# Two decoder layers: up-projection as 512- plus 256-column passes in four banks, banded attention by two heads on the two halves of the array's rows

## The chip, the cores and the metric

The kernel runs on one core of a Trainium2 chip. The time is the device time of one execution in microseconds (us); where several runs are given, their median is used. The engines are named as in the profile: PE is TensorE's matmuls, PEld its weight loads, DVE is VectorE, ACT is ScalarE, POOL is GpSimd, SP is the engine that issues the DMAs.

## The reference, cut to what matters

Batch 1, 256 tokens, model width 2048, two layers, everything in float32.

```
for l in range(2):
    shift_a, scale_a, gate_a, shift_m, scale_m, gate_m = split(silu(c) @ w_ada[l] + b_ada[l])
    h = rms_norm(x, g_pre_mix) * (1 + scale_a) + shift_a
    q_m, k_m, v_m, o_m, i, f, q_a, k_a, v_a = split(h @ w_in)      # one projection
    hm = mlstm(silu(conv(q_m, k_m)), v_m, i, f), normed, * sigmoid(o_m)
    ha = rms_norm(sliding_window_attention(q_a, k_a, v_a, sinks))
    x = x + gate_a * rms_norm(concat(hm, ha) @ w_out)
    h = rms_norm(x, g_pre_mlp) * (1 + scale_m) + shift_m
    x = x + gate_m * rms_norm(relu(h @ w_up)^2 @ w_down)           # 2048 -> 8192 -> 2048
```

The attention has 16 query heads of width 64 and 4 key heads; a query sees the last 128 keys. With blocks of 128 tokens its scores are, for each head, one 128x128 block (first tokens) and one 128x256 block (second tokens against both key blocks); a slope times the distance is subtracted, a sink logit joins the softmax.

## The kernel before, in words

**The split.** A float32 product is made of three products of a rounded type (float32r): each operand is a high part (h, the value rounded) and a low part (l, the rest), and high*high, low*high and high*low are added up in PSUM. Weights come by DMA in loads of 1 MB (`raw`, six buffers, issued by SP in the order of a list `plan`). `split` (lines 222 to 238) makes of half a load one slab: ACT copies 128x1024 into `whi` (line 232), DVE subtracts into `wlo` (line 236). There are four buffers of each, and `prefill` keeps the splits up to three slabs ahead of the matmuls. A slab is two steps of 128 along the contraction (kt) by 512 output columns.

**Units.** `Unit` (lines 287 to 324) is one block of 512 output columns over all kt, with two PSUM banks. PSUM has eight banks: four of `ps_mm` for units and four of `ps_x` for all else, whose users are counted in `live["x"]`; a unit made with `spare=True` takes its banks from `ps_x`. `slabs` issues for each slab the splits ahead, then one step of every open `Task` (`side`), then the slab's matmuls. So side work is bound to the pace of the slabs, each engine working off what it is handed in the order written by the compiler's scheduler. `body_xs` (line 332) keeps activations as the stationary operand and streams 512 weight columns; `body_ws` (line 337) keeps 128 columns of weights and streams the 256 tokens, so a kt step has 4 column groups j with three matmuls of 256 columns each: whi with xh, whi with xl, wlo with xh. Two groups j share a bank.

**Modulation.** `ada_op` (line 198) makes the adaLN values on DVE, one 128x2048 product-and-sum (line 204) for each 1 MB of `w_ada`. `weave` spreads these between the slabs; layer 0's MLP carries 64 of them, layer 1's 32.

**Mixer.** After the projection units for values, keys and queries, `swa` (line 646) runs the attention as a side task while the other projection units (qm, km, vm, om) run. It starts one head per slab, at most four in flight; `swa_head` (line 584) takes one step per slab: scores on the PE (lines 591, 592; 64 partitions, those of the head's half), mask and maxima on DVE (595 to 600), exponentials on ACT (602, 603), three transposes (609), copy (612), the product with the values (618 to 620). Four heads share a PSUM tile `po`, and the next four start when it is done. `mlstm_out` and `concat` wait for the attention's end, and the output projection `op` for `concat`.

**MLP.** `turn` starts the first up units (four in layer 0, two in layer 1) while the norm still runs. Then for each e of 8: `up(2e+2)`, four down units `down(e, c)` of 4 slabs with 512-column matmuls, `up(2e+3)` of 8 slabs (lines 1086 to 1101). `evac_up` (line 1009) takes a finished up unit out of PSUM in two steps: ACT relu and square, DVE square and difference, into the high and low parts that `down` uses one e later.

Of the kernel before, what the change touches and what calls it, by code (L numbers as in the profile page):

```python
# [16 lines left out]
P = 128  # L17
D = 2048
KT = D // P
S = 256  # L20
# [19 lines left out]
def hymba_kernel(ctx: ExitStack, tc: tile.TileContext, x_d, c_d, cols_d, cons_d, wada_d,  # L40
# [243 lines left out]
    def xdone(n=1):  # L284
        live["x"] -= n

    class Unit:


        def __init__(self, name, unit, nk, act, body, spare=False):  # L290
            self.unit, self.nk, self.act, self.body, self.spare = unit, nk, act, body, spare
            self.started = [False, False]
            if spare:
                self.ps = [xalloc(f"{name}_{b}") for b in range(2)]
            else:
                self.ps = [ps_mm.tile([P, 512], F32, tag="mm", name=f"{name}_{b}") for b in range(2)]

# [75 lines left out]
    class PreNorm:  # L373
# [35 lines left out]
        def group(self, g, tok):  # L409

            tag, l = self.tag, self.l
            ada_until(l, self.vsc, self.vsh, n=4 * g + 4)
            if g not in self.groups:
                self.groups[g] = [htp.tile([P, 4, S], F32R, tag=f"ht{a}", name=f"ht{a}{tag}_{g}") for a in "hl"]
            hh, hl = [t[:, :, TK[tok]] for t in self.groups[g]]
# [27 lines left out]
        def modulate(self, e, xnT, hfp):  # L443
# [3 lines left out]
            if g not in self.groups:  # L447
                self.groups[g] = [htp.tile([P, 4, S], F32R, tag=f"ht{a}", name=f"ht{a}{tag}_{g}") for a in "hl"]
            hh, hl = [t[:, 2 * (e % 2):2 * (e % 2) + 2, :] for t in self.groups[g]]
            hf = hfp.tile([P, 2, S], F32, tag="r", name=f"hfs{tag}_{e}")  # L450
# [11 lines left out]
        def __call__(self, kt):  # L462
            hh, hl = self.groups[kt // 4]
            return hh[:, kt % 4, :], hl[:, kt % 4, :]

# [58 lines left out]
    for l in range(DEPTH):  # L524
# [58 lines left out]

        def swa_head(h, po):
            u, hh = h // 8, h % 8
            base, j = 64 * (hh // 4), hh % 4
            qt = fl["qa", u][base:base + 64, j, :]
            kt_ = kaT[base:base + 64, u, :]
            live["w"] += 1
            pss = xalloc(f"pss{L}_{h}")  # L590
            T.matmul(pss[:, 0:P], qt[:, TK[0]], kt_[:, TK[0]], start=True, stop=True)  # L591
            T.matmul(pss[:, P:3 * P], qt[:, TK[1]], kt_, start=True, stop=True)  # L592
            yield
            s = walloc(f"s{L}_{h}", 0)
            V.scalar_tensor_tensor(s, dist, -(2.0 ** (-8.0 * (h + 1) / 16.0)), pss[:, 0:384],
                                   ALU.mult, ALU.add)
            xdone()
            V.tensor_reduce(mx[:, h, 0:1], s[:, 0:P], AX.X, ALU.max)
            V.tensor_reduce(mx[:, h, 1:2], s[:, P:384], AX.X, ALU.max)
            V.tensor_scalar(nm[:, h, :], mx[:, h, :], sk[:, h:h + 1], -1.0, ALU.max, ALU.mult)  # L600
            yield
            A.activation(s[:, 0:P], s[:, 0:P], AF.Exp, bias=nm[:, h, 0:1], accum_out=sm[:, h, 0:1])
            A.activation(s[:, P:384], s[:, P:384], AF.Exp, bias=nm[:, h, 1:2], accum_out=sm[:, h, 1:2])
            yield
            while live["x"] > 3:
                yield
            pt = xalloc(f"pt{L}_{h}")
            for b in range(3):
                T.transpose(pt[:, b * P:(b + 1) * P], s[:, b * P:(b + 1) * P], ident)
            yield  # L610
            sT = walloc(f"sT{L}_{h}", 0)
            A.activation(sT, pt[:, 0:384], AF.Copy)
            xdone()
            yield
            vs = slice((h // 4) * 64, (h // 4) * 64 + 64)
            c0 = (h % 4) * 64
            o0, o1 = po[:, c0:c0 + 64], po[:, 256 + c0:256 + c0 + 64]
            T.matmul(o0, sT[:, 0:P], vat[:, 0, vs], start=True, stop=True)
            T.matmul(o1, sT[:, P:2 * P], vat[:, 0, vs], start=True, stop=False)
            T.matmul(o1, sT[:, 2 * P:3 * P], vat[:, 1, vs], start=False, stop=True)  # L620
            live["w"] -= 1

        def swa_out(g, po):

            hs = slice(4 * g, 4 * g + 4)
            for b in range(2):
                V.tensor_tensor(es[:, hs, b], nm[:, hs, b], sk[:, hs], ALU.add)
            A.activation(es[:, hs, :], es[:, hs, :], AF.Exp)
            V.tensor_tensor(sm[:, hs, :], sm[:, hs, :], es[:, hs, :], ALU.add)
            V.reciprocal(sm[:, hs, :], sm[:, hs, :])  # L630
            yield
            o0 = (g % 2) * 256
            for b in range(2):
                if g % 2 == 0:
                    ha[g // 2, b] = ytile(f"ha{L}_{g // 2}_{b}")
                o = ha[g // 2, b][:, o0:o0 + 256]
                V.tensor_tensor(o.rearrange("p (h d) -> p h d", h=4),
                                po[:, b * 256:b * 256 + 256].rearrange("p (h d) -> p h d", h=4),
                                sm[:, hs, b:b + 1].broadcast_to([P, 4, 64]), ALU.mult)
            xdone()  # L640
            yield
            for b in range(2):
                square_sum(ha[g // 2, b][:, o0:o0 + 256], ssa[:, b, g:g + 1], f"jka{L}_{g}_{b}")
            yield

        def swa():
            while ("qa", 0) not in fl or "kv" not in fl:
                yield
            fly, nxt, outs, po = [], 0, [], None
            while nxt < 16 or fly or outs:  # L650
                for f in list(fly):
                    try:
                        next(f[0])
                    except StopIteration:
                        fly.remove(f)
                        live["q"] -= f[1] % 8 == 7
                        if f[1] % 4 == 3:
                            outs.append(swa_out(f[1] // 4, f[2]))
                            po = None
                for o in list(outs):  # L660
                    try:
                        next(o)
                    except StopIteration:
                        outs.remove(o)
                ok = nxt < 16 and len(fly) < 4 and ("qa", nxt // 8) in fl
                if ok and nxt % 4 == 0:
                    ok = po is None and live["x"] <= 1
                    if ok:
                        po = xalloc(f"po{L}_{nxt // 4}")
# [222 lines left out]
        def concat(i):  # L892
# [8 lines left out]

            hh, hl = [htp.tile([P, 4, S], F32R, tag=f"ht{a}", name=f"ct{a}{L}_{i}") for a in "hl"]
            for q in range(2):
# [105 lines left out]
        def evac_up(un, u):  # L1009
            ps = un.ps  # L1010
            sh, sl = s_tiles(u)
            for b in range(2):
# [8 lines left out]
                yield  # L1021

        def evac_up_tokens(un, u):

# [45 lines left out]

        def evac_down_task(ps, e, c):
            for tok in range(2):
                evac_down(ps, e, c, tok)
            yield

        def down(e, c):
# [4 lines left out]
            if c == 0:  # L1081
                tups[2 * e].finish()
                tups[2 * e + 1].finish()
            return Unit(f"dn{L}_{e}_{c}", ("dn", l, (e, c)), 8, hs, body_xs)

        for e in range(8):
# [5 lines left out]
            for c in range(4):  # L1092
                un = down(e, c)
                if (e, c) == (7, 3):
                    break
                td = Task(evac_down_task(un.run(), e, c))
            if e < 7:
# [108 lines left out]
```

## Time and profile before

| | |
|---|---|
| median of 3 runs | 2267.68 us (2267.40 to 2269.11) |
| the profiled execution | 2270.54 us |
| its span, first to last instruction | 2268.8 us |
| PE / PEld / DVE / ACT busy | 96% / 85% / 74% / 48% of the span |
| chain that ended last: PE / DVE / ACT | 86% / 10% / 2% |
| matmul instructions | 13322 |
| moved from HBM | 586 MB, 259 GB/s over the span |

Read the chain first: it says which engine's work followed on which up to the end. PE's busy time alone says little, since matmuls overlap in the records: a 256-column matmul is recorded with 283 ns, but they start every 120 ns. The spacing of the starts, which the chain gives as a piece's length over its matmuls, is what one costs.

### The profile page before, as it was taken

What the parts mean: (1) busy time and instruction counts of PE and PEld (TensorE: products, weight loads), DVE (VectorE), ACT (ScalarE), POOL (GpSimd) and SP (SyncE); (2) the same over time, 40 slices, a digit from 0 to 9 for tenths busy, and PEclk for the clock granted to TensorE, in tenths of its full rate; (3) what the DMA queues carried; (4) which work ended last, traced back from release to release, by engine and by line L of the source; (5) the groups of instructions that cost most, each with busy time, mean ns of one, the idle gap of its engine ahead of it and who ended that gap; (6) DMA issues with size and microseconds to landing.
All of it is one profiled execution on the core that took longest, in us unless ns stands there. A gap on an engine that the chain in (4) does not pass through costs nothing.

```text
span 2268.8 us, 33092 instructions
## 1 busy us (share of the span) xinstructions
PE 2180.5 (96%) x13322; PEld 1935.3 (85%) x13322; DVE 1688.3 (74%) x2282; ACT 1091.1 (48%) x1533; POOL 1.4 (0%) x14
## 2 busy tenths in 40 slices
PE   6889999899999999999989999989999999999998
PEld 4779777698898998989869988878898998998986
DVE  7988899788788777887577887957556656555556
ACT  4246654645444444434465566546443444444433
POOL 0000000000000000000000000000000000000000
PEclk9999999999999999999999999999999999999999
DMA  9997679488888888888539765745666667555551
GB/s 364 383 364 264 229 299 350 188 343 317 315 303 345 310 308 319 314 317 308 193 118 338 292 236 204 291 172 204 223 223 225 226 225 270 205 186 186 186 188 72
DMA packets 82363, 590.08 MB, mean 260 GB/s; under 512 B 9185, under 2 KB 9633, under 8 KB 10785
## 3 DMA queue, kind: packets, MB, share of 16 engines
q1 hardware_dynamic: 82210, 587.98, 69.6%
q8 instruction: 104, 1.70, 0.3%
q14 instruction: 49, 0.40, 0.1%
HBM read 585.81 MB, written 2.13 MB: 259 GB/s over the span
## 4 chain that ended last, share of the span: by engine, by line
PE 86%; DVE 10%; ACT 2%; issue 1%; DMA 0%; SPq 0%; DVEq 0%; ACTq 0%
PE up L329 32%; PE dn L329 30%; PE op L329 6%; DVE raw L204 4%; PE vm L329 3%; PE om L329 3%; PE qa L329 3%; DVE wlo L236 2%; PE km L329 2%; PE qm L329 2%; PE kva L329 1%; DVE x L388 1%; PE pss L592 1%; PE pss L591 1%; PE psgate L730 0%
## 5 line engine op out<-in xcount | busy, mean ns | idle before, releaser
L236 DVE TENSOR_TENSOR wlo<-raw,whi 128x1024 fp32r<-128x1024 f32 x720 | 876.5, 1223 | 456.8 <-ACT whi L232 455.7
L232 ACT ACTIVATE whi<-raw 128x1024 fp32r<-128x1024 f32 x720 | 758.5, 1058 | 899.1 <-PE dn L329 358.6
L329 PE MATMUL up<-hthm,whi 128*128 128x256 f32 x1920 | 543.6, 283 | 0.0
L329 PE MATMUL up<-hthm,wlo 128*128 128x256 f32 x1920 | 543.3, 283 | 0.0
L329 PE MATMUL up<-htlm,whi 128*128 128x256 f32 x1920 | 543.3, 283 | 0.0
L204 DVE SCALAR_TENSOR_TENSOR raw<-raw,cact 128x2048 f32<-128x2048 f32 x192 | 437.5, 2286 | 8.4 <-DMA raw<-in_wada_dram 8.2
L329 PE MATMUL dn<-whi,sh 128*128 128x512 f32 x1024 | 398.7, 389 | 0.0
L329 PE MATMUL dn<-whi,sl 128*128 128x512 f32 x1024 | 398.6, 389 | 0.0
L329 PE MATMUL dn<-wlo,sh 128*128 128x512 f32 x1024 | 398.4, 389 | 0.0
L329 PEld LDWEIGHTS up<-hthm,whi 128*128 128x128 f32 x1920 | 368.5, 192 | 0.8
L329 PEld LDWEIGHTS up<-htlm,whi 128*128 128x128 f32 x1920 | 368.5, 192 | 0.8
L329 PEld LDWEIGHTS up<-hthm,wlo 128*128 128x128 f32 x1920 | 368.5, 192 | 0.0
L329 PEld LDWEIGHTS dn<-wlo,sh 128*128 128x128 f32 x1024 | 192.2, 188 | 40.1
L329 PEld LDWEIGHTS dn<-whi,sh 128*128 128x128 f32 x1024 | 192.3, 188 | 39.7 <-ACT sh L1036 0.4
L329 PEld LDWEIGHTS dn<-whi,sl 128*128 128x128 f32 x1024 | 192.3, 188 | 39.5 <-DVE sl L1037 0.2
L329 PE MATMUL op<-wlo,cth 128*128 128x512 f32 x256 | 99.6, 395 | 3.1 <-DVE wlo L236 3.0
L329 PE MATMUL op<-whi,cth 128*128 128x512 f32 x256 | 99.3, 396 | 2.4 <-ACT whi L232 2.4
L329 PE MATMUL op<-whi,ctl 128*128 128x512 f32 x256 | 100.2, 393 | 0.0
L329 PE MATMUL vm<-whi,htha 128*128 128x512 f32 x128 | 57.1, 448 | 27.9 <-ACT whi L232 18.0
L1066 DVE TENSOR_TENSOR ys<-ys,dn 128x512 f32<-128x512 f32 x112 | 75.2, 686 | 4.3 <-PE dn L329 4.3
L329 PE MATMUL qa<-htha,whi 128*128 128x256 f32 x256 | 73.2, 286 | 0.0
L329 PE MATMUL qa<-htla,whi 128*128 128x256 f32 x256 | 72.4, 283 | 0.0
(275 smaller groups left out, 2551.3 us busy)
## 6 DMA issues: line engine op xcount, KB each, us to landing
raw<-in_wada_dram SPq DMA_DIRECT2D x192, 1024.0 KB, 6.2
raw<-in_wdn_dram SPq DMA_DIRECT2D x128, 1024.0 KB, 5.1
raw<-in_wup_dram SPq DMA_DIRECT2D x120, 1024.0 KB, 4.9
raw<-in_win_dram SPq DMA_DIRECT2D x56, 1024.0 KB, 5.5
raw<-in_wout_dram SPq DMA_DIRECT2D x32, 1024.0 KB, 6.5
raw<-in_wst_dram SPq DMA_DIRECT2D x16, 1024.0 KB, 7.3
raw<-in_wsu_dram SPq DMA_DIRECT2D x8, 1024.0 KB, 6.8
gp<-gdr SPq DMA_DIRECT2D x4, 1024.0 KB, 4.6
```

Source lines behind the costliest of these rows:

```text
L204: V.scalar_tensor_tensor(w, w, 1.0, cact, ALU.mult, ALU.mult, accum_out=modc[l][:, v, j:j + 1])
L232: A.activation(hi, raw, AF.Copy)
L236: V.tensor_tensor(lo, raw, hi.bitcast(F32), ALU.subtract)
L329: T.matmul(o, a, w, start=not self.started[b], stop=last and i == 2, skip_group_check=True)
L388: V.scalar_tensor_tensor(xc, self.yg[c][tok], r, xc, ALU.mult, ALU.add)
L591: T.matmul(pss[:, 0:P], qt[:, TK[0]], kt_[:, TK[0]], start=True, stop=True)
L592: T.matmul(pss[:, P:3 * P], qt[:, TK[1]], kt_, start=True, stop=True)
L1066: V.tensor_tensor(yt, yt, ps[tok], ALU.add)
```

## The change

In words:

1. Activations' high and low parts lie in one tile, 4 x 2 x 256 per group (`both_parts`), so that for one kt the high and low tokens are 512 adjacent columns. The memory is the same.
2. `body_wide` replaces `body_ws` for the up units made by `up(u)` (12 in layer 0, 14 in layer 1): for each kt and j one 512-column matmul of whi with [xh, xl] and one 256-column matmul of wlo with xh into the first half. Each j has a bank of its own, so a unit has four banks; `up` takes the four of `ps_x` for odd u and for u = 2, else the four of `ps_mm`. The down units with e > 0 and c < 2 take their two from `ps_x`.
3. `evac_up_wide` must add the two halves: per bank ACT copies the second half (256 columns) and DVE adds the first; then DVE makes relu times the value, ACT copies the high part, DVE subtracts.
4. `swa_pair` runs head h and head h+4, whose queries and keys lie on partitions 0 to 63 and 64 to 127, together: both heads' matmuls of the same block follow one another. A pair starts when `live["x"]` is at most 2, at most three pairs are in flight, two pairs share a `po`. `swa_out` and the loop are reordered to match.

```diff
+    def both_parts(name):
+        return htp.tile([P, 4, 2, S], F32R, tag="ht", name=name)
...
+    def body_wide(u, xh, xl, wh, wl, kt):
+        for j in range(4):
+            cs = slice(j * P, (j + 1) * P)
+            T.matmul(u.ps[j], wh[:, cs], u.act.both(kt), start=kt == 0, stop=False, skip_group_check=True)
+            T.matmul(u.ps[j][:, 0:S], wl[:, cs], xh, start=False, stop=kt == u.nk - 1, skip_group_check=True)
...
+        def swa_pair(h, po):
+            u, j, heads = h // 8, h % 4, (h, h + 4)
+            live["w"] += 2
+            pss = [xalloc(f"pss{L}_{g}") for g in heads]
+            for c0, c1, tok, keys in ((0, P, 0, TK[0]), (P, 3 * P, 1, slice(0, S))):
+                for a in range(2):
+                    rows = slice(64 * a, 64 * a + 64)
+                    T.matmul(pss[a][:, c0:c1], fl["qa", u][rows, j, TK[tok]], kaT[rows, u, keys],
+                             start=True, stop=True)
+            yield
+            s = [walloc(f"s{L}_{g}", 0) for g in heads]
+            for a, g in enumerate(heads):
+                V.scalar_tensor_tensor(s[a], dist, -(2.0 ** (-8.0 * (g + 1) / 16.0)), pss[a][:, 0:384],
+                                       ALU.mult, ALU.add)
+                xdone()
+                V.tensor_reduce(mx[:, g, 0:1], s[a][:, 0:P], AX.X, ALU.max)
+                V.tensor_reduce(mx[:, g, 1:2], s[a][:, P:384], AX.X, ALU.max)
+                V.tensor_scalar(nm[:, g, :], mx[:, g, :], sk[:, g:g + 1], -1.0, ALU.max, ALU.mult)
+            yield
...
-                ok = nxt < 16 and len(fly) < 4 and ("qa", nxt // 8) in fl
-                if ok and nxt % 4 == 0:
+                ok = nxt < 8 and len(fly) < 3 and ("qa", nxt // 4) in fl
+                if ok and nxt % 2 == 0:
                     ok = po is None and live["x"] <= 1
...
-                if ok and live["x"] <= 3 and live["w"] <= 6 and po is not None:
-                    f = (swa_head(nxt, po), nxt, po)
+                if ok and live["x"] <= 2 and live["w"] <= 5 and po is not None:
+                    f = (swa_pair(pairs[nxt], po), nxt, po)
...
+        def evac_up_wide(un, u):
+            ps = un.ps
+            sh, sl = s_tiles(u)
+            for b in range(2):
+                r = rp.tile([P, 2, S], F32, tag="r", name=f"r{L}_{u}_{b}")
+                shb = sh[:, 2 * b:2 * b + 2, :]
+                for k in range(2):
+                    A.activation(r[:, k, :], ps[2 * b + k][:, S:2 * S], AF.Copy)
+                for k in range(2):
+                    V.tensor_tensor(r[:, k, :], ps[2 * b + k][:, 0:S], r[:, k, :], ALU.add)
+                if un.spare:
+                    xdone(2)
+                V.scalar_tensor_tensor(r, r, 0.0, r, ALU.max, ALU.mult)
+                A.activation(shb, r, AF.Copy)
+                V.tensor_tensor(sl[:, 2 * b:2 * b + 2, :], r, shb.bitcast(F32), ALU.subtract)
+                yield
...
         def up(u):
-            un = Unit(f"up{L}_{u}", ("up", l, u), KT, hT2, body_ws)
+            un = Unit(f"up{L}_{u}", ("up", l, u), KT, hT2, body_wide, u % 2 == 1 or u == 2, 4)
             un.run()
-            up_done(u, un)
+            tups[u] = Task(evac_up_wide(un, u))
...
-            return Unit(f"dn{L}_{e}_{c}", ("dn", l, (e, c)), 8, hs, body_xs)
+            return Unit(f"dn{L}_{e}_{c}", ("dn", l, (e, c)), 8, hs, body_xs, e > 0 and c < 2)
```

## Rows read from the trace of the kernel before

**Rows 1.** The profile page: span, then busy time, share and instructions by engine.
```profile
span 2268.8 us, 33092 instructions
PE 2180.5 (96%) x13322; PEld 1935.3 (85%) x13322; DVE 1688.3 (74%) x2282; ACT 1091.1 (48%) x1533; POOL 1.4 (0%) x14
```

**Rows 2.** The page's chain that ended last: share of the span by engine.
```profile
PE 86%; DVE 10%; ACT 2%; issue 1%; DMA 0%; SPq 0%; DVEq 0%; ACTq 0%
```

**Rows 3.** The chain in order of time: start us, length us, engine, tile, line, instructions.
```profile
224.23 5.46 PE psgate L730 x48
...
692.02 43.55 PE dn L329 x192
735.57 46.07 PE up L329 x384
```

**Rows 4.** Groups by line and form, ACT and DVE: count, busy us, mean ns, idle before.
```profile
L1015 ACT ACTIVATE r<-up 128x512 f32<-128x512 f32 x60 | 35.2, 588 | 34.7 <-PE up L329 34.3 <-DVE sl L1018 0.4
L1016 ACT ACTIVATE sh<-r 128x512 fp32r<-128x512 f32 x60 | 37.8, 631 | 1.7
L866 ACT ACTIVATE va<-pn 128x256 f32<-128x256 f32 x16 | 6.2, 390 | 0.0
L1063 ACT ACTIVATE ys<-dn 128x512 f32<-128x512 f32 x16 | 9.5, 595 | 9.9 <-PE dn L329 9.9
...
L1017 DVE TENSOR_TENSOR r<-r 128x512 f32<-128x512 f32 x60 | 41.2, 688 | 25.3 <-ACT sh L1016 25.1
L637 DVE TENSOR_TENSOR ha<-po,sm 128x256 f32<-128x256 f32 x16 | 6.5, 416 | 0.8 <-PE po L620 0.6
L709 DVE SCALAR_TENSOR_TENSOR z<-z,e 128x512 f32<-128x512 f32 x8 | 5.4, 681 | 0.7 <-ACT e L705 0.7
```

**Rows 5.** Timeline around one evacuation in layer 0's MLP, ACT, then DVE: start, length, instruction.
```profile
755.64 1.06 ACT L232 ACTIVATE whi<-raw 128x1024 fp32r<-128x1024 f32 x1 [1.82 <-PE up L329]
759.09 1.05 ACT L232 ACTIVATE whi<-raw 128x1024 fp32r<-128x1024 f32 x1
...
758.34 2.29 DVE L204 SCALAR_TENSOR_TENSOR raw<-raw,cact 128x2048 f32<-128x2048 f32 x1
761.15 1.22 DVE L236 TENSOR_TENSOR wlo<-raw,whi 128x1024 fp32r<-128x1024 f32 x1
```

**Rows 6.** Busy us (instructions) by stretch, the two MLPs; then PEclk, DMA share, GB/s.
```profile
450.00:1150.00 700.00, 700.00 (x4447) 638.63 (x4446) 551.68 (x585) 312.05 (x341) 0.00 (x0) 1.00 0.81 303
1600.00:2230.00 630.00, 630.00 (x3993) 574.68 (x3993) 374.06 (x365) 274.18 (x293) 0.00 (x0) 1.00 0.59 211
```

**Rows 7.** The chain in order of time, attention's first heads of layer 0.
```profile
163.70 3.06 PE qm L329 x24
166.77 0.41 PE pss L591 x2
167.18 0.43 PE pss L592 x2
167.62 3.06 PE qm L329 x24
```

**Rows 8.** Timeline of PE and PEld around one head: start, length, instruction, idle before.
```profile
166.70 0.48 PE L591 MATMUL pss<-kaT,qa 64*128 64x128 f32 x2
...
167.55 0.19 PEld L329 LDWEIGHTS qm<-htha,whi 128*128 128x128 f32 x1 [0.33 <-issue]
```

**Rows 9.** Busy us by stretch of 50 us, mixers of layer 0 and 1; columns as Rows 6.
```profile
200.00:250.00 50.00, 50.00 (x337) 42.34 (x337) 46.30 (x82) 36.66 (x66) 0.00 (x0) 1.00 0.61 224
250.00:300.00 50.00, 50.00 (x251) 39.29 (x250) 43.44 (x84) 31.05 (x67) 0.00 (x0) 1.00 0.69 253
300.00:350.00 50.00, 49.28 (x226) 39.06 (x224) 48.15 (x142) 29.35 (x60) 0.00 (x0) 1.00 0.83 314
350.00:400.00 50.00, 46.36 (x199) 35.75 (x199) 49.34 (x67) 17.56 (x26) 0.00 (x0) 1.00 0.92 357
...
1350.00:1400.00 50.00, 50.00 (x238) 38.87 (x237) 42.92 (x95) 33.63 (x63) 0.00 (x0) 1.00 0.56 202
```

More of the change, by code (lines that the diff above doesn't have):

```diff
@@ L287, in hymba_kernel, with __init__ @@
     class Unit:
-        def __init__(self, name, unit, nk, act, body, spare=False):
+        def __init__(self, name, unit, nk, act, body, spare=False, banks=2):
             self.unit, self.nk, self.act, self.body, self.spare = unit, nk, act, body, spare
-            self.started = [False, False]
+            self.started = [False] * banks
             if spare:
-                self.ps = [xalloc(f"{name}_{b}") for b in range(2)]
+                self.ps = [xalloc(f"{name}_{b}") for b in range(banks)]
             else:
-                self.ps = [ps_mm.tile([P, 512], F32, tag="mm", name=f"{name}_{b}") for b in range(2)]
+                self.ps = [ps_mm.tile([P, 512], F32, tag="mm", name=f"{name}_{b}") for b in range(banks)]
         def mm(self, slab, **kw):
@@ L413, in group @@
             if g not in self.groups:
-                self.groups[g] = [htp.tile([P, 4, S], F32R, tag=f"ht{a}", name=f"ht{a}{tag}_{g}") for a in "hl"]
-            hh, hl = [t[:, :, TK[tok]] for t in self.groups[g]]
+                self.groups[g] = both_parts(f"ht{tag}_{g}")
+            hh, hl = [self.groups[g][:, :, a, TK[tok]] for a in range(2)]
             ps = xalloc(f"pst{tag}_{g}_{tok}")
@@ L447, in modulate @@
             if g not in self.groups:
-                self.groups[g] = [htp.tile([P, 4, S], F32R, tag=f"ht{a}", name=f"ht{a}{tag}_{g}") for a in "hl"]
-            hh, hl = [t[:, 2 * (e % 2):2 * (e % 2) + 2, :] for t in self.groups[g]]
+                self.groups[g] = both_parts(f"ht{tag}_{g}")
+            hh, hl = [self.groups[g][:, 2 * (e % 2):2 * (e % 2) + 2, a, :] for a in range(2)]
             hf = hfp.tile([P, 2, S], F32, tag="r", name=f"hfs{tag}_{e}")
@@ L462, in __call__, with both @@
         def __call__(self, kt):
-            hh, hl = self.groups[kt // 4]
-            return hh[:, kt % 4, :], hl[:, kt % 4, :]
+            t = self.groups[kt // 4][:, kt % 4]
+            return t[:, 0, :], t[:, 1, :]
+        def both(self, kt):
+            return self.groups[kt // 4][:, kt % 4].rearrange("p a t -> p (a t)")
     def turn(last_mm, evac, nrm, make, staged=None):
@@ L582, in evac_qa, with by_group @@
             yield
[L584 to L592, printed above, removed]
-            yield
[L594 to L600, printed above, removed]
+        def by_group(t, u, i):
+            return t.rearrange("p (u a i b) c -> p u i a b c", u=2, a=2, i=2, b=2)[:, u, i]
@@ L601, in swa_head @@
             yield
-            A.activation(s[:, 0:P], s[:, 0:P], AF.Exp, bias=nm[:, h, 0:1], accum_out=sm[:, h, 0:1])
-            A.activation(s[:, P:384], s[:, P:384], AF.Exp, bias=nm[:, h, 1:2], accum_out=sm[:, h, 1:2])
+            for a, g in enumerate(heads):
+                A.activation(s[a][:, 0:P], s[a][:, 0:P], AF.Exp, bias=nm[:, g, 0:1], accum_out=sm[:, g, 0:1])
+                A.activation(s[a][:, P:384], s[a][:, P:384], AF.Exp, bias=nm[:, g, 1:2],
+                             accum_out=sm[:, g, 1:2])
@@ L604, in swa_head @@
             yield
-            while live["x"] > 3:
-                yield
-            pt = xalloc(f"pt{L}_{h}")
-            for b in range(3):
-                T.transpose(pt[:, b * P:(b + 1) * P], s[:, b * P:(b + 1) * P], ident)
-            yield
[L611 to L625, printed above, removed]
-            for b in range(2):
[L627 to L639, printed above, removed]
+            for a, g in enumerate(heads):
+                while live["x"] > 3:
+                    yield
+                pt = xalloc(f"pt{L}_{g}")
+                for b in range(3):
+                    T.transpose(pt[:, b * P:(b + 1) * P], s[a][:, b * P:(b + 1) * P], ident)
+                yield
+                sT = walloc(f"sT{L}_{g}", 0)
+                A.activation(sT, pt[:, 0:384], AF.Copy)
+                xdone()
+                yield
+                vs = slice((g // 4) * 64, (g // 4) * 64 + 64)
+                c0 = (2 * a + h % 2) * 64
+                o0, o1 = po[:, c0:c0 + 64], po[:, 256 + c0:256 + c0 + 64]
+                T.matmul(o0, sT[:, 0:P], vat[:, 0, vs], start=True, stop=True)
+                T.matmul(o1, sT[:, P:2 * P], vat[:, 0, vs], start=True, stop=False)
+                T.matmul(o1, sT[:, 2 * P:3 * P], vat[:, 1, vs], start=False, stop=True)
+                live["w"] -= 1
@@ new lines, in swa_out @@
+        def swa_out(g, po):
+            u, i = g // 2, g % 2
+            nmg, smg, esg = [by_group(t, u, i) for t in (nm, sm, es)]
+            skg = sk.rearrange("p (u a i b) -> p u i a b", u=2, a=2, i=2, b=2)[:, u, i]
+            for b in range(2):
+                V.tensor_tensor(esg[:, :, :, b], nmg[:, :, :, b], skg, ALU.add)
+            A.activation(esg, esg, AF.Exp)
+            V.tensor_tensor(smg, smg, esg, ALU.add)
+            V.reciprocal(smg, smg)
+            yield
+            out = []
+            for b in range(2):
+                if i == 0:
+                    ha[u, b] = ytile(f"ha{L}_{u}_{b}")
+                o = ha[u, b].rearrange("p (a i d) -> p i a d", a=2, i=2)[:, i]
+                out.append(o)
+                V.tensor_tensor(o.rearrange("p a (h d) -> p a h d", h=2),
+                                po[:, b * 256:b * 256 + 256].rearrange("p (a h d) -> p a h d", a=2, h=2),
+                                smg[:, :, :, b].unsqueeze(3).broadcast_to([P, 2, 2, 64]), ALU.mult)
@@ L642, in swa_out @@
             for b in range(2):
-                square_sum(ha[g // 2, b][:, o0:o0 + 256], ssa[:, b, g:g + 1], f"jka{L}_{g}_{b}")
+                jk = jkp.tile([P, 512], BF16, tag="jk", name=f"jka{L}_{g}_{b}")
+                A.activation(jk[:, 0:256].rearrange("p (a d) -> p a d", a=2), out[b], AF.Square,
+                             accum_out=ssa[:, b, g:g + 1])
             yield
@@ L648, in swa @@
                 yield
+            pairs = [8 * u + 2 * i + b for u in range(2) for i in range(2) for b in range(2)]
             fly, nxt, outs, po = [], 0, [], None
-            while nxt < 16 or fly or outs:
+            while nxt < 8 or fly or outs:
                 for f in list(fly):
@@ L655, in swa @@
                         fly.remove(f)
-                        live["q"] -= f[1] % 8 == 7
-                        if f[1] % 4 == 3:
-                            outs.append(swa_out(f[1] // 4, f[2]))
+                        live["q"] -= f[1] % 4 == 3
+                        if f[1] % 2:
+                            outs.append(swa_out(f[1] // 2, f[2]))
                             po = None
@@ L664, in swa @@
                         outs.remove(o)
-                ok = nxt < 16 and len(fly) < 4 and ("qa", nxt // 8) in fl
-                if ok and nxt % 4 == 0:
+                ok = nxt < 8 and len(fly) < 3 and ("qa", nxt // 4) in fl
+                if ok and nxt % 2 == 0:
                     ok = po is None and live["x"] <= 1
                     if ok:
-                        po = xalloc(f"po{L}_{nxt // 4}")
-                if ok and live["x"] <= 3 and live["w"] <= 6 and po is not None:
-                    f = (swa_head(nxt, po), nxt, po)
+                        po = xalloc(f"po{L}_{nxt // 2}")
+                if ok and live["x"] <= 2 and live["w"] <= 5 and po is not None:
+                    f = (swa_pair(pairs[nxt], po), nxt, po)
                     next(f[0])
@@ L900, in src @@
                 return va[tok, i - 2][:, k // 2, (k % 2) * P:(k % 2 + 1) * P]
-            hh, hl = [htp.tile([P, 4, S], F32R, tag=f"ht{a}", name=f"ct{a}{L}_{i}") for a in "hl"]
+            ct = both_parts(f"ct{L}_{i}")
+            hh, hl = ct[:, :, 0, :], ct[:, :, 1, :]
             for q in range(2):
@@ L1021, in evac_up @@
                 yield
+        def evac_up_wide(un, u):
+            ps = un.ps
+            sh, sl = s_tiles(u)
+            for b in range(2):
+                r = rp.tile([P, 2, S], F32, tag="r", name=f"r{L}_{u}_{b}")
[10 more added lines that the diff above has]
+                yield
         def evac_up_tokens(un, u):
@@ L1069, in evac_down, with evac_down_task @@
                 V.tensor_tensor(yt, yt, gps[l, GTM][:, CH[c]], ALU.mult)
-        def evac_down_task(ps, e, c):
+        def evac_down_task(un, e, c):
             for tok in range(2):
-                evac_down(ps, e, c, tok)
+                evac_down(un.ps, e, c, tok)
+            if un.spare:
+                xdone(2)
             yield
@@ L1095, in hymba_kernel @@
                     break
-                td = Task(evac_down_task(un.run(), e, c))
+                un.run()
+                td = Task(evac_down_task(un, e, c))
             if e < 7:
```

## The prediction

> **What bounds the kernel now.** I read the page's engine line first [rows 1]: PE is busy 96% of 2268.8 us, DVE 74%. Then the chain [rows 2]: 86% of what ended last is PE's. Then the chain in order of time [rows 3]: in both MLPs, about 1330 us of the span, it is unbroken PE; 384 up matmuls take 46.07 us, 192 down matmuls 43.55 us. So there a nanosecond taken off the spacing of the matmuls comes off the end, and nothing else does. In these stretches DVE is busy 552 of 700 us in layer 0 and 374 of 630 in layer 1, ACT under half, PE all of it at full clock [rows 6]. The mixer is different: PE is busy 50 of 50 us from 200 to 300 in layer 0, but DVE 46.3 and 43.4, and from 300 to 400 DVE works 97.5 of 100 us while PE has gaps [rows 9]. In layer 1's mixer PE leads, DVE 42.9 of 50.
>
> **Up-projection: what a pass costs.** Up streams 256 columns each 46.07/384 = 120.0 ns, down 512 columns each 43.55/192 = 226.8 ns [rows 3]. The difference, 106.8 ns for 256 columns, is 256 columns at 2.4 GHz, the clock granted there. What is left, 13.2 ns at 256 and 13.5 at 512 columns, is a fixed price of a matmul with 128 columns of weights; the gate matmuls with 8 columns of weights, 5.46/48 = 113.8 ns [rows 3], have 7.1. So a site (one kt, one column group) costs 3 x 120.0 = 360.0 ns before and 226.8 + 120.0 = 346.8 after: one fixed price less, 13.2 ns. The weight load of the next pass has at least a 256-column pass to lie beside, as now. Sites: 12 + 14 units x 16 kt x 4 = 1664. **Saved: 1664 x 13.2 ns = 22.0 us**, all on the path. The columns streamed are the same.
>
> The Trainium skill, TensorE: Matmul & The Clock Gate (Back-to-back issue gap), gives a warm gap of N/2.4 + 2.5 ns. By that price a site would go from 327.5 to 325.0 ns, 4 us in all; the measured 120.0 and 226.8 ns do not agree with it, and the sum goes by them.
>
> **Evacuation.** Per half unit ACT has had relu and square, 588 + 631 ns; it gets two 256-column copies and one of 512, by the nearest rows 2 x 390 + 631 = 1411, 0.2 us more [rows 4]. DVE gets two additions of 256 columns from PSUM, 2 x 416 ns; its 512-column square, 688 ns, becomes a product of relu and value, 681 by the nearest row [rows 4], the same. So 0.83 us per half, 1.7 per unit: 12 x 1.7 = 20 us onto 552 of 700 in layer 0, 82% of the shorter stretch; 14 x 1.7 = 24 onto 374 of 630 in layer 1 [rows 6]. No bound on average. In a burst: the slab whose split waits for a free buffer is split as soon as PE is done with an older one (ACT idle 1.82 us until PE, then 755.64; so the next at 758.5). With relu and square between, whi came at 759.09 and wlo at 761.15, done at 762.4 [rows 5]. With four buffers PE wants it three slabs, 3 x 2.88 us, after 758.5, at 767.2: 4.8 us of cover behind the evacuation, an `ada_op` of 2.29 us included. The new evacuation adds 2 x 0.83 us and one more turn between ACT and DVE per half (DVE waits for the copies, ACT for DVE's product), say 1 us each: up to 3.7 us, under 4.8. Cost taken: 0. Below nothing it cannot be, since no work leaves either engine; above, see the rivals.
>
> **Banks.** An odd up has `ps_x`, the next even one `ps_mm`; between a unit's last matmul and the next that wants its banks lies a whole unit or more, with one exception: layer 0's `up(4)` follows `down(0,3)` with nothing between and wants all four `ps_mm`, the last two after two copies of 595 ns on ACT [rows 4]. Its first two column groups run meanwhile (0.7 us). I take 1.0 us lost, between 0 and 2. The task `gate_rows` waits for an `ps_x` place longer; its row is wanted only at e = 7, so nothing. No DMA is added or moved; the loads' queue on SP runs with DMA 81% busy in layer 0's MLP [rows 6], 83% when that is 1.5% shorter.
>
> **Attention.** A slab of 24 matmuls is 24 x 120 = 2.88 us. With one head's scores beside it the slabs follow at 167.62 - 163.70 = 3.92 us [rows 7]: a head costs 1.04 us on PE. The chain splits it: 0.43 us for the two matmuls of 256 columns (each float32 product is two matmuls), so 0.21 for the two of 128; the rest, 0.4 us, lies at the edges: the 0.41 us of the first product holds 0.2 too much, and the slab after it 3.06 against 2.88. The edge is seen in the weight load that follows a head, which starts with its matmul after 0.33 us of idle rather than ahead of it [rows 8]. For a pair before: 2.08 us. After, one pair of edges falls away in any case: 0.40 + 1.28 = 1.68 if the halves of the array don't work together. If they do wholly: 0.40 + 0.64 = 1.04. No row of before shows two row halves at work, so these are the bounds. I take a value between: the records start in program order, and the two matmuls of one product follow one another on the same rows, so only a product's second matmul can run beside the other head's first. In thirds of the way: 107 (first head) + 107 (both) + 213 (the second head's last beside the first's next product) + 213 + 213 = 0.85 us, an estimate. Pair: 1.25 us, saved 0.83, with 8 pairs in a layer **6.6 us of PE per layer** (bounds 3.2 and 8.3).
>
> The Trainium skill, TensorEngine Tiling (Array Packing), says under Key Properties that a change of the tiling mode drains the array, with which the edges in rows 7 and 8 agree, and that tiles run weight loads and matmuls in parallel, which no row shows yet. Its section PSUM Bottleneck speaks against the change: packing speeds TensorE up, not what empties PSUM.
>
> How much of it arrives: DVE's work per head is unchanged, but comes two heads to a slab. Transposes, copies and value products stay one head a slab, four heads still take 8 slabs, so the attention ends at the same slab, and `concat` is not put off. In layer 1 PE leads and DVE has 7 us of 50 in hand [rows 9]: I take 6.0 of 6.6. In layer 0 DVE's hand is 10 us between 200 and 300, and behind it lie 100 us with 2.5 [rows 9]; there a PE that is earlier gains only if DVE gets there earlier too. I take half, 3.3 (bounds 0 and 6.6).
>
> **Sum.** 22.0 + 6.0 + 3.3 - 1.0 = 30.3 us. The profiled execution took 2270.5, its span 2268.8 and 1.7 around it; it lies 2.9 over the median. 2270.5 - 30.3 = 2240.2, less 2.9: **2237.4, say 2237 us** in the median's terms.
>
> **Rivals.**
> 1. *Attention brings nothing, DVE takes its place.* The two-head bursts hold up wlo, and what PE saves in the mixers it waits. For it: DVE at 97.5 of 100 us behind layer 0's attention. Against: layer 1. Time: 2267.7 - 22.0 + 1 = 2247.
> 2. *The halves overlap wholly and both layers pass it on*: 22.0 + 16.6 - 1.0 = 37.6, 2230 us. Against: layer 0's DVE.
> 3. *The fixed price isn't per matmul.* If the 13 ns were exposed weight load, a 256-column pass after a 512-column one could keep what two passes lost, and up would bring little, 0 to 4 us: 2255 to 2259. For it: the gate matmuls with fewer weight columns have 7.1 ns. Against: 512-column passes, with twice the cover, pay 13.5. By the Trainium skill's gap, above, the time would end here too.
> 4. *Slower: the evacuation stalls the splits.* If every turn between ACT and DVE is served in order, a half unit takes 2 x 0.39 + 2 x 0.42 + 0.63 and twice 0.69 (product and difference) = 3.6 us in series [rows 4]; two of them with two wlo (2.4) and two `ada_op`s (4.6) make 14.2 us [rows 5], against two slabs and the cover, 5.5 + 4.8 = 10.3. Where all meet, 4 us of PE are lost; in all 12 units of layer 0, 48 us, the end is 2237 + 48 = 2285. It turns the sign from 30/26 = 1.2 us lost per wide unit. Against: the present order puts wlo between the parts of the evacuation [rows 5], and `ada_op`s come every third slab.
>
> **How the numbers follow.** Forecast, 2232 to 2244: 0.57. Rival 1, or half of it, 2244 to 2252: 0.18. Rival 2, 2226 to 2232: 0.10. Rival 3: 0.08. Rival 4: 0.07, some 2 of these 7 still under the time before. Two in ten left out: 2227 to 2253. A measurement here tells 0.2%, 4.5 us, from no change: faster 0.91, same 0.04, slower 0.05.
>
> **What would show it.** In the chain of the changed kernel an up unit should be 128 matmuls in 22.2 us (23.0 before for 192), with no DVE or ACT piece in the MLPs. Pieces of wlo at the start of a unit mean rival 4; 23 us a unit means rival 3. Two heads' scores should take some 1.05 us of the chain against 1.7; 1.3 and more would mean that the halves don't work together. The mixers tell rival 1: from the first score to op's first matmul, 6 us less in layer 1 and about 3 in layer 0. The prediction falls if PE is no longer the chain in the MLPs.

## The result, and the profile after

The changed kernel takes 2245.20 us (median of 4 runs, 2243.35 to 2246.47) against 2268.23 before (the three runs above and a fourth): a ratio of 0.9898, 95% interval 0.9881 to 0.9915. It is faster by 23.0 us where 30.3 were worked out (2237 us, range 2227 to 2253). The profiled execution has a span of 2243.8 us against 2268.8.

The page after, its head and the chain by engine, to be read against [rows 1] and [rows 2]:

```profile
span 2243.8 us, 29891 instructions
...
PE 2158.0 (96%) x11658; PEld 1842.4 (82%) x11658; DVE 1719.7 (77%) x2386; ACT 1097.5 (49%) x1585; POOL 1.4 (0%) x14
...
PE 84%; DVE 10%; ACT 3%; issue 2%; DMA 1%; SPq 0%; DVEq 0%; ACTq 0%
```

There are 1664 matmuls fewer, one per site, as the sum had it, and PE still leads. The chain in order of time, the stretch of [rows 3] (start, length, engine, tile, line, instructions); the pieces between are the wide units, too many to show:

```profile
594.62 43.53 PE dn L333 x192
...
683.47 43.55 PE dn L333 x192
772.23 43.58 PE dn L333 x192
```

From the end of one e's down units to the start of the next's lie two wide units: 772.23 - (683.47 + 43.55) = 45.21 us, 22.6 a unit. It was 23.03, and 22.2 were forecast. So the merge brought half of what was expected, 0.42 us a unit. From 470 to 1135 us and from 1560 to 2210 us, in the two MLPs, this chain holds PE alone.

Around the first scores, the chain of the changed kernel against [rows 7]:

```profile
160.41 0.86 PE pss L612 x8
161.27 3.06 PE qm L333 x24
164.33 0.86 PE pss L612 x8
```

Two heads take 0.86 us, no longer than one head did before (0.41 + 0.43 plus what lies between). That is the prediction's bound of a whole overlap, 1.04 us with the edges (164.33 - 160.41 - 2.88), not the 1.25 that it took.

Where the time went by stretch, each from the first start of a tile's matmuls to the next in the trace (score = `pss`, op and up their units, the MLP to the last down matmul), in us:

| kernel | to first score, layer 0 | score to op | op to up | MLP | to first score, layer 1 | score to op | op to up | MLP |
|---|---|---|---|---|---|---|---|---|
| before | 162.8 | 159.6 | 112.9 | 725.0 | 89.3 | 182.7 | 100.3 | 724.6 |
| after | 160.3 | 152.6 | 115.4 | 719.8 | 89.3 | 173.6 | 102.4 | 718.9 |

The MLPs gave 5.2 + 5.7 = 10.9 us, the mixers up to op 7.0 + 9.1. The first column differs by 2.5 us for no reason of the change: over all runs below it lies between 158.9 and 162.8 (the two with lighter modulation apart). Layer 0's third column scatters from 111.9 to 115.4, with either attention, and by 2.9 us between two executions of the changed kernel alone (115.4, and 112.5 in e11 below). Its chain here has two waits for weights of `w_out`, 6.95 and 6.93 us long, but of the runs below e10 took 115.4 without such a piece and e2 111.9 with one. What goes with the time is TensorE's granted clock: before the last matmuls of op it falls to half (0.50, 1.2 GHz instead of 2.4) for a short stretch not at all in before, e2, e5 and e11 (111.9 to 112.9 us), once in e3 and e8 (113.5 and 113.8), two or three times in the others (114.8 to 115.4). PE stands in op for about 13 us in all of these, waiting for what comes before it. So this column says nothing against the change.

### The profile page after: what moved, and what is told of

It reads as the page before. It is cut to its first block, busy times and chain, and to the rows that moved or that the text cites. A ratio compares the mean times of both kernels' runs of the same rounds, so it can differ in the third digit from the quotient of the medians.

```text
span 2243.8 us, 29891 instructions
## 1 busy us (share of the span) xinstructions
PE 2158.0 (96%) x11658; PEld 1842.4 (82%) x11658; DVE 1719.7 (77%) x2386; ACT 1097.5 (49%) x1585; POOL 1.4 (0%) x14
## 4 chain that ended last, share of the span: by engine, by line
PE 84%; DVE 10%; ACT 3%; issue 2%; DMA 1%; SPq 0%; DVEq 0%; ACTq 0%
PE dn L333 31%; PE up L352 17%; PE up L353 9%; PE up L333 6%; PE op L333 5%; DVE raw L208 4%; PE om L333 3%; PE vm L333 2%; PE qa L333 2%; DVE wlo L240 2%; PE qm L333 2%; PE km L333 2%; PE kva L333 1%; DVE x L400 1%; DMA raw<-in_wout_dram 1%
## 5 line engine op out<-in xcount | busy, mean ns | idle before, releaser
L352 PE MATMUL up<-htm,whi 128*128 128x512 f32 x1664 | 588.3, 399 | 0.0
L353 PE MATMUL up<-htm,wlo 128*128 128x256 f32 x1664 | 467.5, 281 | 0.0
L352 PEld LDWEIGHTS up<-htm,whi 128*128 128x128 f32 x1664 | 313.2, 188 | 77.1
L353 PEld LDWEIGHTS up<-htm,wlo 128*128 128x128 f32 x1664 | 314.6, 189 | 0.6
L333 PE MATMUL op<-whi,ct 128*128 128x512 f32 x512 | 164.0, 401 | 2.6 <-ACT whi L236 1.8
L333 PE MATMUL vm<-whi,hta 128*128 128x512 f32 x256 | 90.9, 438 | 30.1 <-ACT whi L236 18.6
L333 PEld LDWEIGHTS op<-whi,ct 128*128 128x128 f32 x512 | 97.6, 192 | 25.2 <-ACT whi L236 2.7
L333 PE MATMUL op<-wlo,ct 128*128 128x512 f32 x256 | 101.3, 401 | 2.1 <-DVE wlo L240 2.0
L333 PE MATMUL qa<-hta,whi 128*128 128x256 f32 x512 | 93.6, 285 | 0.0
L333 PE MATMUL up<-htm,whi 128*128 128x256 f32 x512 | 92.8, 284 | 0.0
L333 PEld LDWEIGHTS up<-htm,whi 128*128 128x128 f32 x512 | 80.3, 192 | 0.5
```

What stands on the lines that cost most here:

```text
L333: T.matmul(o, a, w, start=not self.started[b], stop=last and i == 2, skip_group_check=True)
L352: T.matmul(u.ps[j], wh[:, cs], u.act.both(kt), start=kt == 0, stop=False, skip_group_check=True)
L353: T.matmul(u.ps[j][:, 0:S], wl[:, cs], xh, start=False, stop=kt == u.nk - 1, skip_group_check=True)
```

## The experiments

Stretches of the runs that bear on the parts, in us, as in the table above:

| kernel | score to op, layer 0 | op to up | MLP 0 | score to op, layer 1 | op to up | MLP 1 |
|---|---|---|---|---|---|---|
| e1_up_alone | 159.7 | 114.8 | 719.8 | 183.0 | 100.3 | 718.9 |
| e2_attention_alone | 152.6 | 111.9 | 725.0 | 173.6 | 102.4 | 724.6 |
| e3_hi_then_lo | 152.6 | 113.8 | 722.2 | 173.6 | 102.4 | 720.4 |
| e5_256_four_banks | 152.6 | 112.7 | 725.2 | 173.6 | 102.4 | 724.7 |
| e6_light_pairs | 151.3 | 107.4 | 720.2 | 173.3 | 101.6 | 719.0 |
| e7_light_heads | 160.2 | 107.4 | 719.8 | 182.5 | 100.4 | 718.9 |
| e10_kt_groups | 152.6 | 115.4 | 718.4 | 173.6 | 102.4 | 716.6 |
| e9_slab_groups | 152.6 | 115.4 | 717.2 | 173.6 | 102.4 | 715.2 |
| e11_after_again | 152.6 | 112.5 | 719.8 | 173.6 | 102.4 | 718.9 |

**Each part alone.** e1 is the change without its attention hunk, e2 that hunk alone on the kernel before.

> The up-projection part alone: wide passes, four banks, the new evacuation and the joined tiles, with the attention of the kernel before. By the two traces the MLPs gave 5.3 + 5.8 = 11.2 us and the mixers 4.5 + 7.0. If the parts add up, this run is 11 us faster than the kernel before, 2257 us; by the prediction's sum it would be 21, 2247.

> The attention part alone, the up-projection as before. If the parts add up and the mixers' gain is the pairs', it is 11.5 us faster than the kernel before, 2256 to 2257 us; by the prediction 9.3 us, 2259; if the gain of the mixers came from elsewhere (the joined tiles, an earlier start), 2265 or more.

Against 2267.23 us of before on that chip, up alone took 2259.25 us (ratio 0.9958, 0.9941 to 0.9974), attention alone 2254.99 (0.9944, 0.9929 to 0.9959): 8.0 and 12.2 us. The stretches are cleaner than the medians. Up moves the MLPs alone, attention the mixers alone, each by the same amount as in the whole, and the parts add up.

**Why a wide unit costs 22.6 us and not 22.2.** The timeline of PE in a wide unit of the changed kernel, two 512-column passes that lie 20 sites apart, 7.05 us or 353 ns a site:

```profile
640.10 0.40 PE L352 MATMUL up<-htm,whi 128*128 128x512 f32 x1
...
647.15 0.40 PE L352 MATMUL up<-htm,whi 128*128 128x512 f32 x1
```

Three theories: A, changing between 512 and 256 columns costs; B, the joined tokens stream slowly; C, a change of the PSUM bank costs. The first kernel, e3, puts the passes of a kt in two groups:

```diff
         for j in range(4):
             cs = slice(j * P, (j + 1) * P)
             T.matmul(u.ps[j], wh[:, cs], u.act.both(kt), start=kt == 0, stop=False, skip_group_check=True)
+        for j in range(4):
+            cs = slice(j * P, (j + 1) * P)
             T.matmul(u.ps[j][:, 0:S], wl[:, cs], xh, start=False, stop=kt == u.nk - 1, skip_group_check=True)
```

> In the changed kernel a site (512 columns of whi, then 256 of wlo) takes 354 ns in the chain, where 346.8 were worked out: the 512-column pass takes 236 ns instead of the 226.8 that down's take. Here, for each kt, the four 512-column passes come first and the four 256-column ones after them; all else is the changed kernel. Theory A, the alternation of lengths costs the extra: the lengths change twice per kt instead of eight times, so a kt costs about 4 x 346.8 + 8 = 1395 ns instead of 1416, a wide unit 22.3 us instead of 22.65, and 26 units give 9 us: 2236 us. Theory B, the 512-column pass over the joined high and low tokens is slow in itself (what it streams): nothing changes, 2245 us. Theory C, each change of the PSUM bank costs: here the bank changes at each pass, not at every second one, so it gets slower, about 4 x 354 + 4 x 14 = 1470 ns per kt, 2267 us.

The second, e4, streams 512 columns in both passes, `T.matmul(u.ps[j], wl[:, cs], u.act.both(kt), ...)`; the third, e5, has three passes of 256 columns in the same four banks (whi with xh into the first half, whi with xl into the second, wlo with xh into the first).

> As the changed kernel, but the wlo pass also streams the 512 columns of high and low tokens (one more product, low times low, is added). All passes of a wide unit are then 512 columns. Theory A (the alternation of lengths costs): every pass takes 227 ns, 453.6 ns per site. Theory B (the joined tokens stream slowly at 512 columns): 236 ns, 472 per site. Theory C (a change of bank costs): passes take 227 and 241 in turn, 468 per site. The time of the whole is then 1664 x 100 to 118 ns, 166 to 196 us, above the changed kernel's, which says nothing by itself.

> The changed kernel with its four banks, joined tokens and new evacuation, but three passes of 256 columns per site as the kernel before has them (whi with the high, whi with the low, wlo with the high tokens). Theories A and B: every pass takes 120 ns, 360 per site, so a wide unit is 23.0 us again and the whole 26 x 0.38 = 10 us above the changed kernel, 2255 us; this is then what the merge itself is worth. Theory C (a change of bank costs): passes of 120 but 134 where the bank changes, 374 per site, 2279 us. If the new evacuation or the banks cost something by themselves, wlo or ACT pieces appear in the MLPs' chain here too.

Spacing of the starts in the wide units, mean of the trace's records within a kt:

| kernel | passes | spacing, ns | a kt, ns |
|---|---|---|---|
| after | 512, 256 in turn | 236.2, 116.9 | 1412 |
| e3 | four of 512, four of 256 | 234.1, 234.1, 232.1, 228.3, then 117.3 to 119.5 | 1403 |
| e4 | all 512 | 226.7 to 227.2 | 1814 |
| e5 | all 256, four banks | 120.0 | 1440 |

e4 ends B: the joined tokens stream at 226.7 ns when nothing else is between. e5 ends C: with a change of bank at every third pass each takes 120.0; and in e3, with one at each pass, the passes of 256 columns are not slower; nor are those of 512 in e4, with one at every second pass. e5 also shows that four banks and the new evacuation cost nothing, since its MLPs take 725.2 and 724.7 us against 725.0 and 724.6. (One run each: e4 took 2410.81 us, e5 2254.51.) A stands, but e3 recovered less than expected: 9 ns of the 25 lost per kt, not 17. The passes after a change are slow for longer than one pass.

With that in mind the trace of the kernel before can be read again. Its timeline of PE where a down unit follows an up unit (start, length, instruction):

```profile
781.36 0.28 PE L329 MATMUL up<-hthm,wlo 128*128 128x256 f32 x1
781.48 0.40 PE L329 MATMUL dn<-whi,sh 128*128 128x512 f32 x1
...
782.64 0.39 PE L329 MATMUL dn<-wlo,sh 128*128 128x512 f32 x1
...
783.32 0.39 PE L329 MATMUL dn<-wlo,sh 128*128 128x512 f32 x1
```

Five passes from 781.48 to 782.64 take 1.16 us, 232 ns each; the three after it 227. To the nanosecond the records give 234, 235, 229, 232, 231, then 227 and 226, at nearly every such place, and on the way back 113, 119, then 120. So the steady spacings of [rows 3] hold only within a train of equal passes. Coming from a train of 256 columns the first five of 512 cost 27 ns more in all, the way back gives 8.

In e3 the whole was not faster than the change (2248.83 us, ratio 0.9913, 0.9896 to 0.9929, where 2236 were expected), though its slabs were. Its chain shows why, at the end of layer 0's last up unit:

```profile
1102.11 0.94 PE up L352 x4
1103.08 1.07 ACT whi L236
...
1104.17 1.23 DVE wlo L240
1105.39 0.34 DVE r L1067
1105.74 0.04 issue
1105.78 24.34 PE dn L333 x99
```

Unit 15 is followed at once by the down units that need it. With groups all four banks end together, its evacuation starts later, and PE stands, by its records for 2.4 us in each layer. After that the clock is down: the next seven or eight down passes take 427 ns each, at a granted clock of 0.50 (1107 to 1109 us) where the changed kernel has 1.00. The last three runs are built from this reading: groups in all units but 15, by kt (e10) and by slab, eight and eight (e9), and the changed kernel beside them.

```diff
+    def body_slab(u, kt0, hi, lo):
+        for k in range(2):
+            for j in range(4):
+                cs = slice(j * P, (j + 1) * P)
+                T.matmul(u.ps[j], hi[:, k, cs], u.act.both(kt0 + k), start=kt0 + k == 0, stop=False, ...)
+        for k in range(2):
+            for j in range(4):
+                cs = slice(j * P, (j + 1) * P)
+                T.matmul(u.ps[j][:, 0:S], lo[:, k, cs], u.act(kt0 + k)[0], start=False, stop=kt0 + k == u.nk - 1, ...)
...
-            un = Unit(f"up{L}_{u}", ("up", l, u), KT, hT2, body_wide, u % 2 == 1 or u == 2, 4)
+            un = Unit(f"up{L}_{u}", ("up", l, u), KT, hT2, body_wide if u == 15 else body_slab, u % 2 == 1 or u == 2, 4)
```

> Where a train of matmuls of the kernel before goes from 256 to 512 columns (from an up unit to a down unit), the first five 512-column passes take 234, 235, 229, 232 and 231 ns before the spacing settles at 227, and where it goes back to 256 columns the first two take 113 and 119 before 120. The theory now: this price of a change, 27 ns less 8 on the way back, is what the wide unit pays at each site, cut off at the first pass (236 + 117 = 353). From these numbers groups of four and four per kt should take 234+235+229+232 + 113+119+120+120 = 1402 ns; the run with high passes first had 1402.7. Here the passes are grouped by slab, eight of 512 columns and then eight of 256; only unit 15, whose evacuation nothing covers, keeps the turns of the changed kernel. The theory expects 234+235+229+232+231+3 x 227 + 113+119+6 x 120 = 2794 ns per slab against 2825 now: 8 x 31 ns = 0.25 us per unit, 24 units, 6 us: 2239 us. If the price belongs to something else (so many passes whatever their order), it stays at 2245.

> The groups of four and four per kt again, but unit 15 keeps the turns of the changed kernel. With groups everywhere the units' slabs were 20 ns shorter and yet the whole was not faster; in its chain PE stood still for 2 us after unit 15 in each layer, ACT and DVE pieces between it and the last down units, because all four banks end together. If that is where the gain went, this run is about 2 x 2 to 4 us under that one's 2249: 2241 to 2245, 4 us under the changed kernel in the same call. If the loss lay elsewhere, it stays near 2249.

> The changed kernel itself, unaltered, beside the two others on the same chip, since 2 to 6 us are asked: 2243 to 2247 us.

Beside the changed kernel's 2243.10 us, slab groups took 2237.53 (ratio to before 0.9865, 0.9850 to 0.9880) and kt groups 2242.26 (0.9884, 0.9869 to 0.9898). The MLPs gave 2.6 + 3.7 = 6.3 us with slab groups, where 6 were worked out from the spacings of the kernel before, and 1.4 + 2.3 = 3.7 with kt groups, where 4 were expected; that one's median shows only 0.8 of it. (In the profiled executions of both, op to up in layer 0 was 2.9 us longer than in the changed kernel's beside them, at a lower clock, as above.) Against e3, with the same groups, turns in unit 15 gave each MLP 3.8 us back, the stand and the passes at half clock together. The spacings of e9 themselves are those of the kernel before: over some 180 slabs 233.0, 235.9, 228.6, 232.4, 230.5, then 227, and on the way back 112.9, 119.3, then 120, so 2793 ns a slab where 2794 were expected. So the price per change, with its sizes, stands on a forecast that came true. The chain of e9, where two wide units lie between:

```profile
681.80 43.55 PE dn L335 x192
...
770.01 43.55 PE dn L335 x192
```

770.01 - (681.80 + 43.55) = 44.66 us, 22.3 a unit against 22.6.

**How the two heads run.** In e8 the two loops over blocks and heads are exchanged, so that a head's two products are issued before the other head's.

> In the changed kernel the scores of a pair of heads take 0.86 us in the chain, as long as one head's took before: the two halves of the array's rows work side by side wholly, where 1.07 was predicted from a start in program order. Here the pair's matmuls are issued head by head (both products of the first head, then both of the second) instead of in turn. If matmuls start in program order, as the prediction took it, the second head can only begin beside the first head's last matmul: 107 + 107 + 213 + 213, with 107 + 107 of the second beside the last, then 213 + 213, so 1.07 us + 0.2 of the edge = 1.27 us. If each half of the rows works off its own matmuls whatever the order, it stays 0.86 us. If a product's two matmuls are taken apart only between neighbours, something between.

The timeline of PE of e8, then of the changed kernel:

```profile
160.10 0.93 PE L612 MATMUL pss<-kaT,qa 64*128 64x128 f32 x8
```

```profile
164.26 0.93 PE L612 MATMUL pss<-kaT,qa 64*128 64x128 f32 x8
```

The same 0.93 us from the first start to the last end. The records do not name the head. That the exchange reached PE is read from their details: in 14 of the 16 pairs of e8 the second start lies 13 or 14 ns behind the first, in 14 of 16 of the changed kernel 6 to 8 ns, and the semaphore marks on the last two matmuls differ. Two matmuls of one product start 213 ns apart here, so the two that start 13 ns apart must be those of the two heads. The second head's first matmul thus starts 13 ns after the first head's first, while the first head's second, which is issued earlier, starts 213 ns after it. So each half of the rows works off its own matmuls, in both orders tried. One pair of the sixteen, the last of layer 0, has two matmuls of the gates (`pscol`) between its own, in both kernels, and takes 1.55 us. (e8's one time, 2243.66 us, lies among the changed kernel's.)

**Is DVE the bound in layer 0's mixer?** Both kernels multiply only the first half of each modulation load, `V.scalar_tensor_tensor(w[:, 0:1024], w[:, 0:1024], 1.0, cact[:, 0:1024], ...)`: e6 with pairs, e7 with the attention of before.

> The changed kernel with the modulation's products halved in width (1024 of 2048 columns of each load are multiplied and summed; the modulation is therefore not the reference's). DVE has 1.1 us less for each. Read against the next kernel, from the first score matmul to op's first matmul in layer 0. Theory: in layer 0 the pairs gave 4.5 of the 8.3 us that PE saves because DVE is the bound behind the attention; with DVE relieved the pairs are worth 7 to 8.3 us there. Rival: what is lost in layer 0 is lost on PE or ACT (bursts of two heads, waits for PSUM); then it stays near 4.5.

> The kernel with the wide up-projection and the attention of before, with the same halved modulation products (not the reference's either). It is the yardstick of the kernel above it: if DVE was the bound, its layer-0 mixer is 7 to 8.3 us longer than that with pairs, and in layer 1 7 to 8 as well; if not, 4.5 in layer 0.

From score to op the pairs are worth 160.2 - 151.3 = 8.9 us in layer 0 with DVE relieved, 159.7 - 152.6 = 7.1 without (e1 against the changed kernel); one execution each. So DVE does not keep half. The traces show where the 1.8 us lie. From the first score to the attention's last value product (`po`) the pairs gain 135.8 - 127.7 = 8.1 us even without relief. From there to op it is 24.9 us with pairs and 23.9 with single heads, and with DVE relieved 23.9 with either. So 1.0 us is kept behind the attention, where [rows 9] has DVE at 97.5 of 100 us, and a lighter DVE gives it back. The other 0.8 lies inside the attention, 0.3 us shorter with pairs and 0.5 longer with single heads when DVE is relieved; less work on DVE does not explain the second, and it stays open.

In layer 1 the pairs are worth 9.2 against 9.4: nothing is kept. That is more than the 8.3 us that PE saves; 8.2 come up to the last value product, and op's first matmul follows it 1.2 us sooner, but op's matmuls then stretch over 92.9 us instead of 90.8. What layer 1 so gives back, 2.1 us between op and up, shrinks to 1.2 with DVE relieved.

## Right or wrong, step by step

**Direction and range: right, the range in part by luck.** Each part made its own stage faster, and the time lies within the range, 8.2 us above the point. But it lies 1.2 us outside the forecast's own band of 2232 to 2244, in the one given to rival 1, whose mechanism did not occur: the attention brought more than was worked out. The up term came out 11.1 us short, and the attention brought 4.7 us more than taken; that two mis-sized terms offset each other in part is luck.

**The up term: mis-sized, 22.0 us worked out, 10.9 measured.** The step "a site costs 226.8 + 120.0 = 346.8 after" failed. It put two spacings from steady trains next to each other; in turn they cost 236.2 + 116.9 = 353.1 ns within a kt (e4 and e5 give the steady ones back in the same units). The rows of before held the price, at each passage from up to down, but the pieces of [rows 3] average it over 192 passes. Rival 3 saw that up might bring less, but put it down to exposed weight loads. That is not it: in e5 each load has only a 256-column pass to lie beside, and the passes take 120.0 each.

**Evacuation and banks: right in the main.** A cost of 0 for the evacuation is what e5 shows. Around one evacuation the timeline of DVE after has these pieces:

```profile
660.14 1.14 DVE L1065 TENSOR_TENSOR r<-up,r 128x256 f32<-128x256 f32 x3
661.20 0.68 DVE L1068 SCALAR_TENSOR_TENSOR r<-r 128x512 f32<-128x512 f32 x1
661.80 1.23 DVE L240 TENSOR_TENSOR wlo<-raw,whi 128x1024 fp32r<-128x1024 f32 x1
662.95 0.68 DVE L1070 TENSOR_TENSOR sl<-r,sh 128x512 fp32r<-128x512 f32 x1
```

Each addition takes about 0.4 us as costed, and wlo runs between the parts, which is what spoke against rival 4. The 1.0 us for the first wait on four banks did not show. The chain has `down(0,3)` here:

```profile
528.47 43.85 PE dn L333 x192
```

From its end, 528.47 + 43.85, to the next down at 594.62 are 22.3 us, no more than a wide unit.

**Attention: the step on program order failed, upwards.** The pair costs 0.40 + 0.64 us, rival 2's price, not 0.40 + 0.85: by e8 matmuls on the two halves do not wait for their turn in the program, where the prediction had them wait. The share that arrives was mis-sized as well: of 8.3 us of PE per layer, 7.0 arrive in layer 0 (3.3 taken), and in layer 1 9.1 up to op less 2.1 given back, 7.0 (6.0 taken). Together 14.0 against 9.3. That DVE holds something back in layer 0 is shown by e6 and e7, at 1.0 us behind the attention. That the attention ends at the same slab was right: from the first score to the last value product PE runs 588 matmuls of the projection units in layer 0 and 660 in layer 1, before and after.

The Trainium skill, TensorEngine Tiling (Array Packing), Key Properties, has tiles run weight loads and matmuls in parallel; the traces agree, with 0.86 us for two heads as for one.

**The sum.** 10.9 + 14.0 = 24.9 us against 31.3 worked out for the two parts. The medians give 23.0 here and 25.2 where e11 ran beside the kernel before; the start and layer 0's op stretch scatter by 3 to 4 us each.

## What to carry to other kernels

A spacing taken from a long train of equal matmuls is not the price of such a matmul in another order: look in the trace for a place where the two kinds already meet, and price the change from there. Here passes of equal length belonged in groups, as long as what waits for the last of them had cover: where it had none, PE's stand also cost it the clock for the next passes. Two 64-row products on the two halves of the array's rows cost what one did, 0.86 us, in both orders in which they were issued; and two heads then pay the 0.40 us at the edges once instead of twice.

## What had not been expected of the hardware

After a change from a train of 256 columns to 512 the spacing takes five passes to settle (234, 235, 229, 232, 231, then 227 ns), at full granted clock (1.00 in both MLPs, [rows 6]). Weight loads do not show why: those of the second to fifth pass start some 0.23 us before their pass and take 0.19 us. Behind the alternating unit of the changed kernel the down passes take ten to settle (medians 241, 237, 233, 236, 225, 230, 235, 229, 232, 231, then 226 or 227). The cause stays open.

Matmuls on different halves of the rows do not start in the order of the program: by the reading of e8 above, one issued after three others of the other half (its second pass of 128 columns and both of 256) started 200 ns before the first of them.
